# Gated linear attention block with a convolutional FFN: the gated product stored as four plain blocks, its sums formed by accumulating DMAs

## The chip, the cores and the metric

The kernel runs on one core of a Trainium2 chip. The metric is the device time of one execution in microseconds (us). Engines are called as in the profile: PE (matmuls) and PEld (its weight loads), DVE (vector), ACT (scalar), POOL (general vector), SP (an engine that here only issues DMAs). All data is float32.

## The reference

One layer over x of 2048 tokens by 1024 features: a gated linear attention mixer, then the FFN, each with a normalisation ahead of it and a residual behind it. The change lies in the FFN:

```python
def conv_ffn(h, w_up, conv_w, conv_b, w_down):       # h: 2048 x 1024
    u = causal_dwconv(h @ w_up, conv_w, conv_b)      # w_up: 1024 x 5632, 3 taps per feature
    g, val = jnp.split(u, 2, axis=-1)                # 2816 features each
    return (jax.nn.silu(g) * val) @ w_down           # w_down: 2816 x 1024

x = x + conv_ffn(rmsnorm(x, ffn_norm_w), ...)
return rmsnorm(x, final_norm_w)
```

## The kernel before, in words

Every large product is made of float32 operands that are split in two parts: `split` (L186 to L189) lets ACT cast the high part and DVE subtract it for the low part. `mm3p` (L174) then issues three matmuls of 128x512 for one block (L179, L180, L181). On top of that, each product of matrices is done as a fast 2x2 block product: seven products p1 to p7 of sums of blocks in place of eight.

The up stage (`phase_u`, ahead of and around L1237 to L1347) makes u = h @ w_up, the convolution, the gate and the gated product. Tokens come in two halves s of 1024, features in 11 pairs of tiles f; a half and a pair make a group of 7 products x 2 f = 14 jobs, each of 12 matmuls. There are 2 x 11 x 14 = 308 jobs, 3696 matmuls. One PSUM bank (`a`) collects p1, then p6, p7 and p4 of the same f on top of it, and ACT copies the intermediate states out: `copied` (L1237) copies p1 (tile c1) and p6 (c2), L1333 copies p7 (c3), L1340 copies p4. The next product into that bank waits for the copy. `conv` (L1247) forms the convolution on ACT (L1253) and DVE (L1255), `gated` (L1260) multiplies gate and value on DVE (L1262).

While the first half is worked on, the operands of the second half are prepared in steps (`prep_h2`, L820 ff.): each step makes the high and low part of a sum (tiles `h2p`, cast at L188, and stored from ACT at L841 into scratch `hd`), and at the change of halves SP loads them as `h_p` (L904). The tiles `h2p` (two per step), the c3 copies and the sums of the gated product share one ring of six buffers, tag "as" (AB = 6).

`gated` at an odd f has four quadrants of the pair: a11 and a21 (even f, two token quarters), a12 and a22 (odd f). It stores three of them plainly from SP and has POOL form four sums (L1276 add, L1280, L1278 and L1280 subtract) into the ring, each stored by SP (L1282). So scratch `ad` holds the seven operands of the down stage: 7 x 256 KB for each pair and half.

The down stage (L1351 ff.) runs 14 units, products p1, p5, p6, p7, p2, p4, p3, each for both halves; a unit has 11 steps q of 12 matmuls. Per step, SP loads a tile `da` of `ad` (`load_step`, 10 steps ahead of the matmuls, into a ring of four pairs of tiles), and `prep_step` splits it (tiles `da`, 4 steps ahead). In the unit of the first half the step also has weight blocks: SP loads them (L1380, tiles `dwr`, and L1357's `ch`), POOL sums them up (L1406 and L1408), and they are split into `dw_p`. The results go onto xs tiles, the residual rows, which SP loads during the first two units (L1464, 16 loads of 512 KB) and which DVE and POOL add to (L1489 to L1511). Final normalisation and output stand in the units p4 and p3 (L1466 to L1482).

A planner's clock decides when the delayed pieces (steps of `prep_h2`, weight preparation) are put into the code, and a scheduler orders each engine's instructions.

Of the kernel before, what the change touches and what calls it, by code (L numbers as in the profile page):

```python
# [10 lines left out]
F32 = mybir.dt.float32  # L11
# [3 lines left out]
ALU = mybir.AluOpType  # L15

P = 128
# [8 lines left out]
def hybrid_kernel(  # L26
# [17 lines left out]
    nc = tc.nc  # L44
    x = x[0]
# [19 lines left out]
    AB = 6  # L65
# [18 lines left out]
    NS = S // TS  # L84
    TT = TS // P
    PAIRS = TT // 2
    OPS = ("p1", "p5", "p6", "p7", "p4", "p2", "p3")

    PORD = ("p1", "p5", "p6", "p2", "p7", "p3", "p4")
    NQ = NF // 2  # L90
    ULEAD = 5
    DLEAD = 4
    DLOAD = 6
    DWLOAD = 3

    cst = ctx.enter_context(tc.tile_pool(name="cst", bufs=1))
    gx = ExitStack()
# [12 lines left out]
    pools = {}  # L110

    def scratch(shape, name):
        return dr.tile(shape, F32, tag=name, name=name)
# [7 lines left out]
    wsd = {(ps_, o, k): scratch([P, 2, 512], f"ws_{ps_}_{o}_{k}") for ps_ in "BY" for o in ("p5", "p6", "p7", "p3") for k in range(2)}  # L121
    b12d = [scratch([P, 512], f"b12_{j}") for j in range(NP)]
    hd = {(s, o, j): scratch([P, 2, 512], f"hd_{s}_{o}_{j}") for s in range(NS) for o in OPS for j in range(PAIRS)}
    ad = {(s, o, q): scratch([P, 512], f"ad_{s}_{o}_{q}") for s in range(NS) for o in OPS for q in range(NQ)}

    def mm_ps(name):
        return ps.tile([P, 512], F32, tag="mm", name=name, bufs=4)
# [4 lines left out]
    def raw_tile(shape, name):  # L132
        return wr.tile(shape, F32, tag="raw", name=name, bufs=RB)
# [757 lines left out]
    done = {"rows": 0}  # L891
# [290 lines left out]
    def tiles2(ap):  # L1182

        v = ap.rearrange("p (j c k) -> p c j k", c=2, k=P)
        return v[:, 0], v[:, 1]

    def tiles1(ap):
        return ap.rearrange("p (j k) -> p j k", k=P)
# [3 lines left out]
    def phase_u():  # L1192
        raws, wops, sums, made = {}, {}, {}, {}
# [46 lines left out]
        def new_u(s, i, f):  # L1240
            c = f + i * NF
            u = pools["us"].tile([P, TS + 2], F32, tag="u", name=f"u_{s}_{c}", bufs=3)
            nc.gpsimd.tensor_copy(u[:, 0:2], halo[:, c, :])
            made["u", i, f] = u
            return tiles2(u[:, 2:2 + TS])
# [14 lines left out]
        def gated(s, f):  # L1260
            t, v = made.pop(("t", 0, f)), made.pop(("t", 1, f))
            nc.vector.tensor_mul(t, t, v)  # L1262
            made["a", f % 2] = tiles2(t)
            q = f // 2
            if f % 2 == 0:
                nc.sync.dma_start(tiles1(ad[s, "p1", q]), made["a", 0][0])
                return
            (a11, a21), (a12, a22) = made["a", 0], made["a", 1]
            nc.sync.dma_start(tiles1(ad[s, "p2", q]), a12)
            nc.sync.dma_start(tiles1(ad[s, "p4", q]), a22)  # L1270
            last = None
            for o, fn, x, y in (("p5", "add", a21, a22), ("p6", "sub", None, a11), ("p3", "rsub", None, a12), ("p7", "sub", a11, a21)):
                t = pools["us"].tile([P, 512], F32, tag="as", name=f"as_{s}_{q}_{o}", bufs=AB)
                tv = tiles1(t)
                if fn == "add":
                    nc.gpsimd.tensor_add(tv, x, y)  # L1276
                elif fn == "rsub":
                    nc.gpsimd.tensor_sub(tv, y, last)  # L1278
                else:
                    nc.gpsimd.tensor_sub(tv, last if x is None else x, y)  # L1280
                last = tv
                nc.sync.dma_start(ad[s, o, q], t)  # L1282

        load(0, 0)
        load(0, 1)
# [1 line left out]
        done = 0  # L1287
        bank = {}
        for k, (s, g, o, f) in enumerate(jobs):
# [23 lines left out]
            if o == "p1":  # L1313
                a = bank["a", f] = mm_ps(f"ua_{s}_{f}")
# [5 lines left out]
            elif o == "p6":  # L1320
                a = bank["a", f]
                mm3p(a, pairs, first=False, more=True)
                made["u2", f] = copied(f"c2_{s}_{f}", a)
            elif o == "p2":
                pb = mm_ps(f"ub_{s}_{f}")
                mm3p(pb, pairs)
                ev, _ = new_u(s, 0, f)
                nc.vector.tensor_add(ev, tiles1(pb), tiles1(made.pop(("p1", f))))  # L1328
            elif o == "p7":
                a = bank["a", f]  # L1330
# [6 lines left out]
            elif o == "p4":  # L1337
                a = bank.pop(("a", f))
# [3 lines left out]
            else:  # L1342
                c = bank.pop(("c", f))
                mm3p(c, pairs, first=False, more=True)
                _, od = tiles2(made["u", 0, f][:, 2:2 + TS])
# [5 lines left out]
    units = [(o, s) for o in ("p1", "p5", "p6", "p7", "p2", "p4", "p3") for s in range(NS)]  # L1351
    steps = [(o, s, q) for o, s in units for q in range(NQ)]
    araw, wraw, aops, wops, chain, xs, acc, wgrp = {}, {}, {}, {}, {}, {}, {}, {}
    dstep = {"loaded": 0, "wloaded": 0, "done": 0}

    def blocks_of(o):
        return {"p1": (), "p5": ((1, 2),), "p6": ((2, 2),), "p7": ((2, 2), (1, 2)), "p2": ((2, 1),), "p4": ((2, 1),), "p3": ((2, 2),)}[o]  # L1357
# [16 lines left out]
    def load_wr(k):  # L1374
        o, s, q = steps[k]
        if s == 0:
            wraw[o, q] = []
            for ij in blocks_of(o):
                r = next(dstep["wr"])
                nc.sync.dma_start(r, block(q, *ij))  # L1380
                wraw[o, q].append(r)

    def load_step(k):
        o, s, q = steps[k]
        if k % 2 == 0:
            araw["tile"] = raw_tile([P, 2, 512], f"da_{o}_{s}_{q}")
        r = araw["tile"][:, k % 2, :]
        nc.sync.dma_start(r, ad[s, o, q])
        araw[o, s, q] = r

    def w_slots(o, q):
        if q % 4 == 0:
            wgrp[o] = slots(("p7", "p4", "p3")[q // 4], f"dw_{o}_{q}")
        return wgrp[o][q % 4 * 2:][:2]
# [22 lines left out]
    def d_load(n):  # L1417
        while dstep["wloaded"] < min(len(steps), n - DLOAD + DWLOAD):
            load_wr(dstep["wloaded"])
            dstep["wloaded"] += 1  # L1420
        while dstep["loaded"] < min(len(steps), n):
            load_step(dstep["loaded"])
            dstep["loaded"] += 1

    def d_prep(n):
        while dstep["done"] < min(len(steps), n):
            prep_step(dstep["done"])
            dstep["done"] += 1
# [55 lines left out]
    def use(o, s, m, pb, nw):  # L1484

        e, d = s * TT + 2 * m, s * TT + 2 * m + 1
        c1, c2 = slice(0, 512), slice(512, 1024)
        xe, xd = xs[e], xs[d]
        add = nc.vector.tensor_add  # L1489
        if o == "p1":  # L1490
            acc[s, m] = dx.tile([P, 512], F32, tag=f"acc{s}_{m}", name=f"acc_{s}_{m}")
            nc.scalar.copy(acc[s, m], pb)
            add(xe[:, c1], xe[:, c1], pb)
        elif o == "p5":
            add(xd[:, c2], xd[:, c2], pb)
            add(xe[:, c2], xe[:, c2], pb)
        elif o == "p6":
            add(acc[s, m], acc[s, m], pb)
            nc.gpsimd.tensor_add(xe[:, c2], xe[:, c2], acc[s, m])
        elif o == "p7":  # L1500
            add(acc[s, m], acc[s, m], pb)
            nc.gpsimd.tensor_add(xd[:, c1], xd[:, c1], acc[s, m])
            nc.gpsimd.tensor_add(xd[:, c2], xd[:, c2], acc[s, m])
        elif o == "p2":
            add(xe[:, c1], xe[:, c1], pb)
        elif o == "p4":
            add(xd[:, c1], xd[:, c1], pb)
            final_tile(d, nw)
        else:
            add(xe[:, c2], xe[:, c2], pb)  # L1510
            final_tile(e, nw)  # L1511

    nwf = dx.tile([P, D], F32, tag="nwf", name="nwf")
    more = [dx.tile([P, 512], F32, tag=f"wr{i}", name=f"dwr_{i}") for i in range(2 * (DWLOAD + 1) - len(dstep["wr"]))]
    dstep["wr"] = itertools.cycle(dstep["wr"] + more)
    for n, (o, s) in enumerate(units):
        banks = [(mm_ps if n % 2 == 0 else aux_ps)(f"pd_{o}_{s}_{m}") for m in range(PAIRS)]
        last = n + 1 == len(units)
# [8 lines left out]
        for q in range(NQ):  # L1527
            k = n * NQ + q
# [43 lines left out]
```

## Time and profile before

| | |
|---|---|
| time, 3 runs | 2183.61 us median, 2178.07 to 2184.76 |
| span of the profiled execution | 2176.4 us |
| mean granted clock of TensorE in it | 0.986 |
| up stage (first matmul into the second stage's) | 851.9 to 1743.0 us |
| down stage, matmuls | 1743.0 to 2167.9 us |
| stores of the gated product and its sums | 154 of 256 KB |
| loads of the down stage's operands | 154 of 256 KB |

The span lies 7.2 us below the median of the runs and 1.7 us below the lowest; it leaves out what lies ahead of the first and behind the last instruction. How to read the profile: busy time is summed by engine; a wait is put down to the instruction that released it last; the chain of waits follows the work that ended last back from its end. A window row gives the length, then busy time and count for PE, PEld, DVE, ACT and POOL, the granted clock, the busy share of the 16 DMA engines and GB/s.

### The profile page before, as it was taken

Reading aid. Unit: us, or ns where it says so; the run is one execution under the profiler, and the core shown is the slowest. Engines: PE = TensorE matmul, PEld = TensorE weight load, DVE = VectorE, ACT = ScalarE, POOL = GpSimd, SP = SyncE. Lnnn points to the kernel's source line nnn. Section 1 sums busy time; section 2 is a strip of 40 time slices with the busy share of each in tenths; the row PEclk is TensorE's granted clock in tenths of the full one; section 3 lists DMA queues with packets and bytes.
Section 4 is the critical chain, followed back from the end, with each engine's and each line's share of the span. In section 5 each row is a group of like instructions: output and inputs, shape, how many; then the busy total and the mean of one; then the engine's idle time right before and its main releaser. Section 6 shows DMA issues by size and latency. Waiting matters only on the chain.

```text
span 2176.4 us, 28914 instructions
## 1 busy us (share of the span) xinstructions
PE 2086.0 (96%) x9832; PEld 1730.6 (80%) x9832; DVE 1648.3 (76%) x2168; ACT 1104.3 (51%) x2024; POOL 734.9 (34%) x606
## 2 busy tenths in 40 slices
PE   7999999989998999799999998999999999999998
PEld 5788788878887887677888777888888877888886
DVE  8756888798888663778899776988888776457564
ACT  5555756665565775444554453554445533333342
POOL 2000011111111002456666554666565444037010
PEclk9999999999999999999999999999999999999999
DMA  6646684578557999654453458242424567254453
GB/s 219 223 165 211 213 297 137 159 229 298 178 195 251 323 344 365 207 163 131 146 184 102 146 177 291 88 131 76 139 77 124 187 247 269 97 184 160 141 182 113
DMA packets 305124, 411.76 MB, mean 189 GB/s; under 512 B 23742, under 2 KB 160110, under 8 KB 304976
## 3 DMA queue, kind: packets, MB, share of 16 engines
q1 hardware_dynamic: 267440, 346.99, 48.2%
q10 hardware_dynamic: 37536, 62.93, 8.6%
q8 instruction: 77, 1.26, 0.2%
q14 instruction: 71, 0.58, 0.1%
HBM read 266.70 MB, written 143.13 MB: 188 GB/s over the span
## 4 chain that ended last, share of the span: by engine, by line
PE 65%; DVE 13%; DMA 10%; issue 6%; ACT 2%; POOL 2%; SPq 0%; ACTq 0%; DVEq 0%; POOLq 0%
PE pd_p L180 5%; PE pd_p L181 5%; PE pd_p L179 5%; PE ua L179 5%; PE ua L180 5%; PE ua L181 5%; DVE t L1255 4%; DMA h_p<-hd_p 2%; PE uc L179 2%; PE uc L181 2%; PE uc L180 2%; PE mp_Y L180 2%; PE mp_Y L181 2%; PE mp_Y L179 2%; PE mp_R L179 2%
## 5 line engine op out<-in xcount | busy, mean ns | idle before, releaser
L179 PE MATMUL ua<-h_p,uw_p 128*128 128x512 f32 x704 | 279.0, 396 | 28.0 <-ACT c L1237 23.2
L1255 DVE SCALAR_TENSOR_TENSOR t<-u,cw,t 128x1024 f32<-128x1024 f32 x176 | 270.4, 1542 | 10.3 <-ACT t L1253 9.1
L180 PE MATMUL ua<-h_p,uw_p 128*128 128x512 f32 x704 | 277.7, 394 | 0.0
L181 PE MATMUL ua<-h_p,uw_p 128*128 128x512 f32 x704 | 277.2, 394 | 0.0
L180 PE MATMUL pd_p<-dw_p,da 128*128 128x512 f32 x616 | 240.7, 391 | 3.4 <-DVE da L189 3.4
L181 PE MATMUL pd_p<-dw_p,da 128*128 128x512 f32 x616 | 240.3, 390 | 0.0
L179 PE MATMUL pd_p<-dw_p,da 128*128 128x512 f32 x616 | 240.1, 390 | 0.0
L189 DVE TENSOR_TENSOR da<-da_p,da 128x512 fp32r<-128x512 f32 x154 | 131.4, 906 | 105.4 <-ACT da L188 105.3
L189 DVE TENSOR_TENSOR uw_p<-ur,uw_p 128x512 fp32r<-128x512 f32 x176 | 168.6, 979 | 48.8 <-ACT uw_p L188 48.4
L188 ACT CAST da<-da_p 128x512 fp32r<-128x512 f32 x154 | 85.3, 619 | 207.9 <-PE pd_p L181 149.9
L179 PEld LDWEIGHTS ua<-h_p,uw_p 128*128 128x128 f32 x704 | 134.4, 191 | 59.6 <-ACT c L1237 31.8
L188 ACT CAST uw_p<-us 128x512 fp32r<-128x512 f32 x132 | 82.1, 622 | 169.0 <-POOL us L1217 130.7
L189 DVE TENSOR_TENSOR uw_p<-us,uw_p 128x512 fp32r<-128x512 f32 x132 | 127.9, 978 | 47.8 <-ACT uw_p L188 46.8
L181 PEld LDWEIGHTS ua<-h_p,uw_p 128*128 128x128 f32 x704 | 134.5, 191 | 28.6
L180 PEld LDWEIGHTS ua<-h_p,uw_p 128*128 128x128 f32 x704 | 134.5, 191 | 27.9
L180 PEld LDWEIGHTS pd_p<-dw_p,da 128*128 128x128 f32 x616 | 116.0, 188 | 28.7 <-DVE da L189 4.7
L179 PE MATMUL uc<-h_p,uw_p 128*128 128x512 f32 x352 | 137.2, 390 | 0.9 <-DVE u L1328 0.9
L679 POOL TENSOR_TENSOR r<-r,gnw 128x512 f32<-128x512 f32 x32 | 46.9, 1466 | 268.6 <-ACT r L678 228.2
L181 PE MATMUL uc<-h_p,uw_p 128*128 128x512 f32 x352 | 136.9, 389 | 0.0
L180 PE MATMUL uc<-h_p,uw_p 128*128 128x512 f32 x352 | 136.9, 389 | 0.0
L181 PEld LDWEIGHTS pd_p<-dw_p,da 128*128 128x128 f32 x616 | 116.1, 188 | 24.1
L179 PEld LDWEIGHTS pd_p<-dw_p,da 128*128 128x128 f32 x616 | 116.1, 188 | 24.0
(278 smaller groups left out, 5474.8 us busy)
## 6 DMA issues: line engine op xcount, KB each, us to landing
ur<-in_ffn_w_up_dram SPq DMA_DIRECT2D x168, 256.0 KB, 3.7
da_p<-ad_p SPq DMA_DIRECT2D x154, 256.0 KB, 3.8
h_p<-hd_p SPq DMA_DIRECT2D x56, 512.0 KB, 8.0
ad_p<-as_p SPq DMA_DIRECT2D x88, 256.0 KB, 2.3
ad_p<-t SPq DMA_DIRECT2D x66, 256.0 KB, 3.1
x<-in_x_dram SPq DMA_DIRECT2D x32, 512.0 KB, 4.7
ch<-in_ffn_w_down_dram SPq DMA_DIRECT2D x61, 256.0 KB, 4.2
hr_A_p<-h1d_p SPq DMA_DIRECT2D x56, 256.0 KB, 3.0
```

The source lines that it names most:

```text
L179: nc.tensor.matmul(ps_ap, ah, bl, start=(first and i == 0), stop=False, **kw)
L180: nc.tensor.matmul(ps_ap, al, bh, start=False, stop=False, **kw)
L181: nc.tensor.matmul(ps_ap, ah, bh, start=False, stop=(last and i == len(pairs) - 1), **kw)
L188: nc.scalar.copy(hi, src)
L189: nc.vector.tensor_sub(lo, src, f32(hi))
L679: nc.gpsimd.tensor_mul(r, r, sp["gnw"])
L1255: nc.vector.scalar_tensor_tensor(t, u[:, k:k + TS], cw[:, k, c:c + 1], t, op0=ALU.mult, op1=ALU.add)
```

## The change

`gated` no longer makes sums. Every f stores its two quadrants plainly, so `ad` holds a11, a21, a12 and a22 from the up stage: four stores for a pair, and no POOL operation.

In the down stage, `load_step` loads the first addend. `add_step`, two steps behind the loads, lets POOL issue a DMA from `ad` into the same tile with the operation "add" (`accum_op`): p5 is a21 += a22, p6 is p5 += a11, p7 is a11 += a21, p3 is p6 += a12. `keep_step`, four steps behind the loads, stores the finished p5 and p6 back into `ad` from SP, since p6 and p3 start from them. The signs differ from before (all four are plain sums), and five operations in `use` become subtractions.

```diff
+    DADD = 2
+    DKEEP = 4
...
         def gated(s, f):
             t, v = made.pop(("t", 0, f)), made.pop(("t", 1, f))
             nc.vector.tensor_mul(t, t, v)
-            made["a", f % 2] = tiles2(t)
-            q = f // 2
-            if f % 2 == 0:
-                nc.sync.dma_start(tiles1(ad[s, "p1", q]), made["a", 0][0])
-                return
-            (a11, a21), (a12, a22) = made["a", 0], made["a", 1]
-            nc.sync.dma_start(tiles1(ad[s, "p2", q]), a12)
-            nc.sync.dma_start(tiles1(ad[s, "p4", q]), a22)
-            last = None
-            for o, fn, x, y in (("p5", "add", a21, a22), ("p6", "sub", None, a11), ("p3", "rsub", None, a12), ("p7", "sub", a11, a21)):
-                t = pools["us"].tile([P, 512], F32, tag="as", name=f"as_{s}_{q}_{o}", bufs=AB)
...
-                nc.sync.dma_start(ad[s, o, q], t)
+            for o, part in zip((("a11", "a21"), ("a12", "a22"))[f % 2], tiles2(t)):
+                nc.sync.dma_start(tiles1(ad[s, o, f // 2]), part)
...
+    ASRC = {"p1": ("a11",), "p5": ("a21", "a22"), "p6": ("p5", "a11"), "p7": ("a11", "a21"), "p2": ("a12",), "p4": ("a22",), "p3": ("p6", "a12")}
...
-        nc.sync.dma_start(r, ad[s, o, q])
+        nc.sync.dma_start(r, ad[s, ASRC[o][0], q])
         araw[o, s, q] = r
+
+    def add_step(k):
+        o, s, q = steps[k]
+        for other in ASRC[o][1:]:
+            nc.gpsimd.dma_start(araw[o, s, q], ad[s, other, q], accum_op=ALU.add)
+
+    def keep_step(k):
+        o, s, q = steps[k]
+        if o in ("p5", "p6"):
+            nc.sync.dma_start(ad[s, o, q], araw[o, s, q])
...
     def d_load(n):
...
+        for what, fn, late in (("added", add_step, DADD), ("kept", keep_step, DKEEP)):
+            while dstep[what] < min(len(steps), n - late):
+                fn(dstep[what])
+                dstep[what] += 1
```

On ACT, in the third group of the first half, the order before has two steps of the second half's operands (the casts into `h2p` and their stores) ahead of and between the two c2 copies of tiles f = 4 and 5:

```order
L188 CAST h2p_4_p6_0_10254<-h2r_4_0_9820 128x512
L188 CAST uw_0_4_p2_10337<-ur_0_4_1_10053 128x512
L841 DMA hd_1_p6_0_322<-h2p_4_p6_0_10254 128x512
L841 DMA hd_1_p6_0_322<-h2p_4_p6_1_10255 128x512
L188 CAST h2p_4_p2_0_10343<-h2r_4_1_9822 128x512
L1237 COPY c2_0_4_10335<-ua_0_4_10240 128x512
L188 CAST uw_0_5_p2_10358<-ur_0_5_1_10056 128x512
L841 DMA hd_1_p2_0_334<-h2p_4_p2_0_10343 128x512
L841 DMA hd_1_p2_0_334<-h2p_4_p2_1_10344 128x512
L1237 COPY c2_0_5_10356<-ua_0_5_10264 128x512
```

At the same place afterwards (line numbers are larger by two, and L1317 is the c3 copy) the rows are:

```order
L190 CAST uw_0_5_p4_10276<-ur_0_5_1_10023 128x512
L190 CAST uw_0_4_p2_10293<-ur_0_4_1_10020 128x512
L1239 COPY c2_0_4_10291<-ua_0_4_10196 128x512
L190 CAST uw_0_5_p2_10314<-ur_0_5_1_10023 128x512
L1239 COPY c2_0_5_10312<-ua_0_5_10220 128x512
```

The casts into `h2p` no longer stand between the c2 copies. On SP, in the second unit of the down stage, the order before is the loads of p5's operands, the xs rows and then the weight blocks `dwr`:

```order
L1464 DMA xs_13_16850<-x1d_13_91 128x1024
L1388 DMA da_p5_0_4_16845<-ad_0_p5_5_358 128x512
L1464 DMA xs_14_16868<-x1d_14_92 128x1024
L1388 DMA da_p5_0_6_16883<-ad_0_p5_6_359 128x512
L1464 DMA xs_15_16891<-x1d_15_93 128x1024
L1388 DMA da_p5_0_6_16883<-ad_0_p5_7_360 128x512
L1380 DMA dwr_0_16517<-in_ffn_w_down_dram 128x512
```

Afterwards the same stretch holds the stores of the sums (L1386), each of which waits for its accumulating DMA:

```order
L1386 DMA ad_0_p5_0_386<-da_p5_0_0_16508 128x512
L1465 DMA xs_13_16590<-x1d_13_91 128x1024
L1374 DMA da_p5_0_4_16583<-ad_0_a21_5_358 128x512
L1386 DMA ad_0_p5_1_387<-da_p5_0_0_16508 128x512
L1465 DMA xs_14_16610<-x1d_14_92 128x1024
L1374 DMA da_p5_0_6_16625<-ad_0_a21_6_359 128x512
L1386 DMA ad_0_p5_2_388<-da_p5_0_2_16544 128x512
L1465 DMA xs_15_16635<-x1d_15_93 128x1024
L1374 DMA da_p5_0_6_16625<-ad_0_a21_7_360 128x512
L1386 DMA ad_0_p5_3_389<-da_p5_0_2_16544 128x512
L1366 DMA dwr_0_16253<-in_ffn_w_down_dram 128x512
```

The load of step 5 now stands behind the store of step 0, and the first weight block behind the store of step 3. On POOL the accumulating DMAs (L1381) stand in one queue with the weight sums (L1403):

```order
L1381 DMA da_p5_0_2_16544<-ad_0_a22_3_378 128x512
L1403 TENSOR_TENSOR ch_0_16023<-ch_1_16024,ch_0_16023 128x512 x2
L1381 DMA da_p5_0_4_16583<-ad_0_a22_4_379 128x512
L1381 DMA da_p5_0_4_16583<-ad_0_a22_5_380 128x512
L1381 DMA da_p5_0_6_16625<-ad_0_a22_6_381 128x512
L1381 DMA da_p5_0_6_16625<-ad_0_a22_7_382 128x512
L1403 TENSOR_TENSOR ch_0_16023<-dwr_0_16253,ch_0_16023 128x512
```

The weight sum that uses the first block `dwr` stands behind the accumulating DMA of step 7.

More of the change, by code (lines that the diff above doesn't have):

```diff
@@ L123, in hybrid_kernel @@
     hd = {(s, o, j): scratch([P, 2, 512], f"hd_{s}_{o}_{j}") for s in range(NS) for o in OPS for j in range(PAIRS)}
-    ad = {(s, o, q): scratch([P, 512], f"ad_{s}_{o}_{q}") for s in range(NS) for o in OPS for q in range(NQ)}
+    ad = {(s, o, q): scratch([P, 512], f"ad_{s}_{o}_{q}") for s in range(NS) for o in ("a11", "a21", "a12", "a22", "p5", "p6") for q in range(NQ)}
     def mm_ps(name):
@@ L1262, in gated @@
             nc.vector.tensor_mul(t, t, v)
-            made["a", f % 2] = tiles2(t)
-            q = f // 2
-            if f % 2 == 0:
-                nc.sync.dma_start(tiles1(ad[s, "p1", q]), made["a", 0][0])
-                return
-            (a11, a21), (a12, a22) = made["a", 0], made["a", 1]
-            nc.sync.dma_start(tiles1(ad[s, "p2", q]), a12)
-            nc.sync.dma_start(tiles1(ad[s, "p4", q]), a22)
-            last = None
-            for o, fn, x, y in (("p5", "add", a21, a22), ("p6", "sub", None, a11), ("p3", "rsub", None, a12), ("p7", "sub", a11, a21)):
-                t = pools["us"].tile([P, 512], F32, tag="as", name=f"as_{s}_{q}_{o}", bufs=AB)
[L1274 to L1282, printed above, removed]
+            for o, part in zip((("a11", "a21"), ("a12", "a22"))[f % 2], tiles2(t)):
+                nc.sync.dma_start(tiles1(ad[s, o, f // 2]), part)
         load(0, 0)
@@ L1353, in hybrid_kernel @@
     araw, wraw, aops, wops, chain, xs, acc, wgrp = {}, {}, {}, {}, {}, {}, {}, {}
-    dstep = {"loaded": 0, "wloaded": 0, "done": 0}
+    dstep = {"loaded": 0, "wloaded": 0, "done": 0, "added": 0, "kept": 0}
+    ASRC = {"p1": ("a11",), "p5": ("a21", "a22"), "p6": ("p5", "a11"), "p7": ("a11", "a21"), "p2": ("a12",), "p4": ("a22",), "p3": ("p6", "a12")}
     def blocks_of(o):
@@ L1488, in use @@
         xe, xd = xs[e], xs[d]
-        add = nc.vector.tensor_add
+        add, sub = nc.vector.tensor_add, nc.vector.tensor_sub
         if o == "p1":
@@ L1495, in use @@
             add(xd[:, c2], xd[:, c2], pb)
-            add(xe[:, c2], xe[:, c2], pb)
+            sub(xe[:, c2], xe[:, c2], pb)
         elif o == "p6":
-            add(acc[s, m], acc[s, m], pb)
+            sub(acc[s, m], acc[s, m], pb)
             nc.gpsimd.tensor_add(xe[:, c2], xe[:, c2], acc[s, m])
@@ L1501, in use @@
             add(acc[s, m], acc[s, m], pb)
-            nc.gpsimd.tensor_add(xd[:, c1], xd[:, c1], acc[s, m])
-            nc.gpsimd.tensor_add(xd[:, c2], xd[:, c2], acc[s, m])
+            nc.gpsimd.tensor_sub(xd[:, c1], xd[:, c1], acc[s, m])
+            nc.gpsimd.tensor_sub(xd[:, c2], xd[:, c2], acc[s, m])
         elif o == "p2":
```

## The prediction

> **What bounds the kernel now.** I read the busy times first, then windows by stage, then the waits and the chains in the windows where matmuls are missing. The page says which engine the span belongs to:
>
> ```profile
> span 2176.4 us, 28914 instructions
> PE 2086.0 (96%) x9832; PEld 1730.6 (80%) x9832; DVE 1648.3 (76%) x2168; ACT 1104.3 (51%) x2024; POOL 734.9 (34%) x606
> ```
>
> PE is busy for 96% of the span, and the change leaves its matmuls as they are. So the change can only win stalls of PE and the slow matmuls behind a stall, or add some. Where they are, the windows show (length; busy and count of PE, PEld, DVE, ACT, POOL; granted clock; DMA share; GB/s):
>
> ```profile
> core 0: us, PE busy (x) PEld busy (x) DVE busy (x) ACT busy (x) POOL busy (x), PEclk, DMA share, GB/s
> 880.00:930.00 50.00, 43.37 (x179) 35.31 (x178) 38.07 (x39) 21.91 (x34) 24.33 (x21) 0.92 0.59 184
> 930.00:1330.00 400.00, 383.40 (x1660) 314.69 (x1659) 339.64 (x334) 197.78 (x300) 242.36 (x196) 0.98 0.50 158
> 1330.00:1380.00 50.00, 43.98 (x184) 35.68 (x183) 35.36 (x33) 21.77 (x34) 24.61 (x18) 0.93 0.57 176
> 1380.00:1730.00 350.00, 350.00 (x1546) 289.91 (x1545) 300.35 (x281) 173.54 (x260) 206.37 (x147) 1.00 0.37 113
> 1730.00:1830.00 100.00, 96.60 (x417) 78.91 (x416) 75.33 (x73) 40.90 (x69) 46.46 (x28) 0.98 0.75 271
> 1774.00:1806.00 32.00, 31.00 (x137) 25.37 (x136) 14.85 (x20) 9.23 (x17) 3.37 (x2) 1.00 1.02 389
> 1830.00:1930.00 100.00, 100.00 (x443) 82.80 (x442) 54.49 (x84) 31.12 (x57) 19.26 (x14) 1.00 0.49 161
> ```
>
> From 1380 to 1730 (second half of the up stage) nothing stalls: 1546 matmuls in 350 us, 4.417 per us at clock 1.00. Against that rate 880 to 930 lacks 42 matmuls (9.5 us), 930 to 1330 lacks 107 (24.2 us), 1330 to 1380 lacks 37 (8.4 us). In the down stage 1730 to 1830 lacks 26 against the 443 of 1830 to 1930 (5.9 us). The stretch 1774 to 1806 inside it is the only one where the DMA engines are full (share 1.02, 389 GB/s).
>
> **What PE waits for in the first half.** The waits from 918 to 1362 (total, times, longest):
>
> ```profile
> PE ua L179 <- ACT c L1237: 23.2, 8, 6.6
> ACT h2p_p L188 <- DMA ad_p<-as_p: 11.7, 3, 5.5
> ACT h2p_p L188 <- DMA hd_p<-h2p_p: 11.0, 2, 5.6
> PE ub L179 <- DMA h_p<-hd_p: 5.1, 1, 5.1
> ```
>
> PE waits for the ACT copies that free its bank. ACT is late because a cast into h2p stands ahead of the copy and waits for a ring buffer: three times for the store of a POOL sum (`as`), twice for the store of an earlier h2p. The chain into the stall at 1011 has the whole mechanism:
>
> ```profile
> 1004.54 1.67 POOL as_p L1276
> 1006.28 1.64 POOL as_p L1280
> 1007.93 2.26 DMA ad_p<-as_p
> 1010.21 0.62 ACT h2p_p L188
> 1010.83 0.49 ACT c L1237
> 1011.37 0.80 PE ua L179
> ```
>
> The second half prepares no h2p and has no such wait, though POOL forms the same sums there. The h_p wait is the change of halves:
>
> ```profile
> 1331.12 1.67 POOL as_p L1276
> 1336.19 1.71 POOL as_p L1280
> 1337.92 0.32 SPq L1282
> 1340.28 7.39 DMA h_p<-hd_p
> 1347.87 0.77 PE ub L179
> ```
>
> SP issues in order; the loads of h_p stand behind four stores that wait for four POOL sums.
>
> **Part 1: the sums leave the up stage.** What goes away on POOL and on SP:
>
> ```profile
> L1276 POOL TENSOR_TENSOR as_p<-t,t 128x512 f32<-128x512 f32 x22 | 36.8, 1673 | 26.6 <-DVE t L1262 26.6
> L1280 POOL TENSOR_TENSOR as_p<-as_p,t 128x512 f32<-128x512 f32 x22 | 35.7, 1621 | 1.7
> L1280 POOL TENSOR_TENSOR as_p<-t 128x512 f32<-128x512 f32 x22 | 35.4, 1609 | 0.0
> L1278 POOL TENSOR_TENSOR as_p<-t,as_p 128x512 f32<-128x512 f32 x22 | 35.4, 1609 | 1.6
> ad_p<-as_p SPq DMA_DIRECT2D x88, 256.0 KB, 2.3
> ad_p<-t SPq DMA_DIRECT2D x66, 256.0 KB, 3.1
> ```
>
> That is 143 us of POOL and 66 of 154 stores (88 plain ones remain). By themselves they are worth nothing, since POOL and DMA have room (POOL 242 of 400 us, DMA share 0.50 in 930 to 1330). What counts is the ring: four of its tiles per group disappear, so a cast into h2p no longer waits for `ad_p<-as_p`, and it finds a buffer that was released several steps earlier, which covers the 5.6 us waits for `hd_p<-h2p_p` too. The order after also has the casts out from between the c2 copies. At the change of halves h_p no longer waits for 1331.12 to 1337.9, four sums of 1.7 us, so it lands some 6 us earlier; the wait was 5.1.
>
> The loss there is 24.2 + 8.4 = 32.6 us. What is late next are the copies behind ordinary ACT and DVE work, which in the second half cost nothing; I leave 3.6 us for what remains and take **29 us**. Lower bound 18: half of the 24.2 (the three `as` waits are about half of the five) and 6 of the 8.4. Upper bound 36: all, and 3 of the 9.5 us before 930. That first stall I otherwise leave in, for the order ahead of it is unchanged.
>
> **Part 2: the sums enter the down stage's DMA.** Loads stay 154. New are 88 accumulating DMAs (22 each for p5, p6, p7, p3) and 44 stores of kept sums. The units p5 to p7 (66 steps) carry 66 and 44 of these, and this is where the rows are tight:
>
> ```profile
> 1743.02 0.39 PE L179 MATMUL pd_p<-dw_p,da 128*128 128x512 f32 x1
> 1784.53 0.32 SPq L1388 DMA_DIRECT2D da_p<-ad_p  x1
> xs<-x1d SPq DMA_DIRECT2D x16, 512.0 KB, 8.3
> ```
>
> A step is 12 / 4.417 = 2.717 us. The matmuls of p1 start at 1743.0 and take 22 steps, so p5 starts at 1802.8 and p7 ends at 1982.1. The first operand of p5 is loaded at 1784.53. Splitting lies ahead of the matmuls, so the last operand of p7 must be there about 8 us before its end: a window of 190 us. A 256 KB tile costs the full engines 262,144 / 389,000 = 0.674 us. Work in the window: 70 loads (four of them p2's, ahead), 44 kept sums and 48 weight blocks are 162 tiles, 109.2 us; nine xs rows (seven issued after 1784.53, two in flight) and the final norm's weights, 20 tiles in all, 13.5 us. Sum 122.7 us, to which 66 accumulating DMAs come at A each.
>
> No accumulating DMA is in this trace. Lower bound of A: one pass like a load, 0.674. Upper bound: three passes (read, read again, write, each like a transfer), 2.02. I take two passes, 1.35: nearest to a load and a store of the same tile, since source and old value are both read and the result written once. Then 122.7 + 89.0 = 211.7, 22 us over the window. Before has already lost 5.9 us at this place, so **16 us** are new. At 0.674 the sum is 167 and fits; at 2.02 it is 256, and 60 us are new.
>
> The Trainium skill speaks against the change here: "Collectives: The Full Stack", section "The bandwidth ceiling: the fold count and why AG ≠ RS ≠ AR", says that a reduction in the DMA engine pushes two source reads through the same read ring and so runs at about half the rate of a copy (measured ratio 1.93). As an estimate from that page, A would be 0.674 x 1.93 = 1.30, the new loss about 13 us and the time 2167; no run yet shows it.
>
> **Part 3: order and waits.** `keep_step` has SP wait for an accumulating DMA, and behind it are queued the next load, the xs rows and the weight blocks. The weight blocks matter most, since the stall at 1823 follows from them:
>
> ```profile
> 1799.49 7.74 DMA dwr<-in_ffn_w_down_dram
> 1807.30 1.29 POOL ch L1406
> 1813.60 3.79 DMA dwr<-in_ffn_w_down_dram
> 1823.56 0.79 PE pd_p L180
> ```
>
> The first block moves behind the store of step 3's sum. That step's load was issued near 1790 and takes about 8 us; its accumulating DMA then needs between 4 and 8, which gives an issue at 1802 to 1806 in place of 1799.5. SP's silence meanwhile empties the queue, which returns a part. Priced alone: 2 to 8 us, taken 4; beside the 16 us above it is the same lateness and not counted again.
>
> Issuing from POOL costs between 0.32 us (SP's issue) and 1.67 us (a POOL sum). 66 of them are 21 to 110 us in 180; POOL is busy for 19 of 100 us from 1830 on, so even the upper end is covered there. Turning five additions of `use` into subtractions, and the stage p3 with its 22 accumulations but only 11 weight blocks, I cost at nothing: PE's lead over 22 steps (60 us) covers 22 x (0.674 + 1.35) + 7.4 = 52 us.
>
> **Sum.** Profiled execution: 2176.4 - 29 + 16 = 2163; it lies 7.2 us below the median of the runs, so **2171 us** against 2183.6.
>
> **Rivals.**
>
> *The accumulation is as cheap as a load* (A up to about 1.0). For it: outside 1774 to 1806 the share is 0.49, the engines have room. Then only part 3's 4 us remain: 2183.6 - 29 + 4 = 2159. Chance 0.33.
>
> *The DMA becomes the bound of the down stage* (slower than before). Mechanism: in p5 to p7 each tile takes three passes, loads and kept sums wait, and PE waits for `da`. It decides from 66 A = 190 - 122.7 + 5.9 + 29, A = 1.55; at 2.02 the time is 2183.6 - 29 + 60 = 2215. For it: the loaded queue at 1784 to 1806 already gives 8 us per load, and a load of step 5 now follows a finished accumulation of step 0. Against: from 1830 on half the engines' time is free. Chance 0.20.
>
> *The up stage keeps half of its stalls.* Two of five h2p waits were for `hd_p<-h2p_p`, not for a sum; if the ring only rotates to the next such wait, the gain is 14: 2183.6 - 14 + 16 = 2186. Against: the second half with the same sums and no h2p is free of stalls, and the ring now has four tiles fewer per group. Chance 0.12.
>
> **How the numbers follow.** The forecast (A near two passes) has 0.35. A measurement of this kernel can tell about 0.3%, 6.5 us. Faster by more: nearly all of the first rival (0.32), three quarters of the forecast (0.26): 0.58. Within: 0.07 of the forecast, 0.06 of the half gain, 0.03 of the dear accumulation just above its turning point: 0.16. Slower: the rest, 0.26. The range goes from 2153 (cheap accumulation with some 34 us of gain) to 2206 (A about 1.9); the forecast's own range is 2162 to 2180.
>
> **What would show it.** Up stage: the waits `PE ua <- ACT c` of the first half under 4 us, no wait for `h_p`, and 930 to 1330 with about 1750 matmuls. Down stage: a DMA share near 1.0 from 1784 up to about 1970, PE waiting for `da` or `dw` by some 20 us, and the busy time of the queue that POOL issues on, divided by 88 and by a load's, gives A. The forecast is wrong if that ratio is near 1 or 3, if c copies still wait for h2p casts, or if PE waits for POOL while the DMA engines are idle.

## The result, and the profile after

The changed kernel takes 2192.66 us (median of 5 runs, 2190.66 to 2196.57) against 2178.07 us for the kernel before beside it: ratio 1.0065, 95% interval 1.0048 to 1.0082, slower by 14.6 us. Forecast were 2171 us, faster. The time lies inside the stated range, on the wrong side. The times of all runs are medians; that of e5 leaves out two of its ten executions, of 2591 and 8690 us.

The up stage did what was forecast, and more. From 918 to 1362 the copies that free PE's bank hold PE for 0.6 us, where they held it for 23.2:

```profile
PE ua L181 <- ACT c L1239: 0.6, 1, 0.6
```

The first matmul of the down stage, at 1743.02 before, is now here:

```profile
1704.08 0.39 PE L181 MATMUL pd_p<-dw_p,da 128*128 128x512 f32 x1
```

That is 38.9 us earlier. The windows of the changed kernel (same columns as before) show where the gain and the loss lie:

```profile
880.00:930.00 50.00, 47.99 (x205) 39.20 (x204) 39.62 (x42) 25.74 (x40) 23.63 (x20) 0.97 0.53 159
930.00:1330.00 400.00, 400.00 (x1767) 331.31 (x1766) 330.48 (x352) 207.14 (x312) 188.92 (x167) 1.00 0.50 156
1330.00:1380.00 50.00, 49.39 (x218) 40.60 (x217) 38.56 (x42) 27.60 (x42) 19.13 (x17) 1.00 0.45 127
1774.00:1830.00 56.00, 50.48 (x207) 40.53 (x206) 30.32 (x36) 15.95 (x28) 28.39 (x26) 0.94 0.99 271
1830.00:1930.00 100.00, 76.63 (x305) 59.80 (x303) 40.40 (x51) 24.68 (x43) 37.18 (x38) 0.90 0.92 239
1930.00:1980.00 50.00, 43.09 (x170) 34.72 (x171) 28.78 (x29) 12.80 (x23) 31.59 (x31) 0.90 0.96 241
```

From 930 to 1330 PE is busy all the time, with the 1767 matmuls of the full rate. The loss is in the units p5 to p7: 305 matmuls where 443 fit, at a clock of 0.90, with the DMA engines at 0.92 (from 1830 to 1930). The page has a queue that was not there:

```profile
span 2189.3 us, 28925 instructions
...
q0 software_dynamic: 12672, 23.07, 6.3%
...
da_p<-ad_a POOLq DMA_DIRECT2D x88, 256.0 KB, 5.8
```

The 88 accumulating DMAs took 6.3% of 2189.3 us, so 1.57 us of all 16 engines each. From 1830 to 1930 both queues can be compared (packets, MB, share):

```profile
q1 hardware_dynamic: 9078, 16.53, 46.8%
q0 software_dynamic: 4032, 7.34, 44.8%
```

16.53 MB are 63 plain tiles, 0.742 us each; 7.34 MB are 28 accumulating ones, 1.60 us each. And SP, which loads, waits (1800 to 1980, its own queue; then PE from 1743 on):

```profile
SPq L1386 <- DMA da_p<-ad_a: 71.8, 29, 6.4
```

```profile
PE pd_p L181 <- ACT da L190: 20.3, 8, 8.1
PE pd_p L182 <- DVE da L191: 18.1, 7, 5.8
```

SP spends 71.8 of 180 us waiting with a store of a kept sum for the accumulation, and PE waits for the split of the operands that SP then loads late.

### The profile page after: what moved, and what is told of

The parts are those of the page before. It is cut to its first block, busy times and chain, and to the rows that moved or that the text cites. A ratio compares the mean times of both kernels' runs of the same rounds, so it can differ in the third digit from the quotient of the medians.

```text
span 2189.3 us, 28925 instructions
## 1 busy us (share of the span) xinstructions
PE 2091.3 (96%) x9832; PEld 1732.0 (79%) x9832; DVE 1563.8 (71%) x2168; ACT 1111.3 (51%) x2024; POOL 647.0 (30%) x606
## 4 chain that ended last, share of the span: by engine, by line
PE 65%; DMA 12%; DVE 10%; issue 6%; POOL 2%; ACT 2%; SPq 1%; ACTq 0%; DVEq 0%; POOLq 0%
PE ua L181 6%; PE ua L182 6%; PE ua L183 6%; DMA da_p<-ad_a 5%; PE uc L181 3%; PE uc L183 3%; PE uc L182 3%; PE pd_p L182 3%; PE pd_p L181 3%; PE pd_p L183 3%; PE mp_Y L183 2%; PE mp_Y L182 2%; PE mp_Y L181 2%; PE mp_R L181 2%; PE mp_R L182 2%
## 5 line engine op out<-in xcount | busy, mean ns | idle before, releaser
L181 PE MATMUL pd_p<-dw_p,da 128*128 128x512 f32 x616 | 246.1, 400 | 20.3 <-ACT da L190 20.3
L182 PE MATMUL pd_p<-dw_p,da 128*128 128x512 f32 x616 | 246.1, 400 | 18.1 <-DVE da L191 18.1
L1257 DVE SCALAR_TENSOR_TENSOR t<-u,cw,t 128x1024 f32<-128x1024 f32 x176 | 254.1, 1446 | 11.4 <-ACT t L1255 10.4
L183 PE MATMUL pd_p<-dw_p,da 128*128 128x512 f32 x616 | 244.9, 398 | 0.0
L191 DVE TENSOR_TENSOR uw_p<-ur,uw_p 128x512 fp32r<-128x512 f32 x176 | 123.1, 716 | 73.5 <-ACT uw_p L190 68.4
L191 DVE TENSOR_TENSOR uw_p<-us,uw_p 128x512 fp32r<-128x512 f32 x132 | 121.8, 932 | 63.7 <-ACT uw_p L190 63.3
L181 PEld LDWEIGHTS pd_p<-dw_p,da 128*128 128x128 f32 x616 | 118.9, 193 | 48.5 <-ACT da L190 23.7
L182 PEld LDWEIGHTS pd_p<-dw_p,da 128*128 128x128 f32 x616 | 119.1, 193 | 46.9 <-DVE da L191 21.9
L1255 ACT ACTIVATE t<-u,cw 128x1024 f32<-128x1024 f32 x88 | 109.8, 1248 | 58.7 <-DVE u L1330 58.6
L183 PEld LDWEIGHTS pd_p<-dw_p,da 128*128 128x128 f32 x616 | 118.7, 193 | 24.8
```

The source lines that it names most:

```text
L181: nc.tensor.matmul(ps_ap, ah, bl, start=(first and i == 0), stop=False, **kw)
L182: nc.tensor.matmul(ps_ap, al, bh, start=False, stop=False, **kw)
L183: nc.tensor.matmul(ps_ap, ah, bh, start=False, stop=(last and i == len(pairs) - 1), **kw)
L191: nc.vector.tensor_sub(lo, src, f32(hi))
L1255: nc.scalar.activation(t, u[:, 2:2 + TS], AF.Identity, scale=cw[:, 2, c:c + 1], bias=cw[:, 3, c:c + 1])
L1257: nc.vector.scalar_tensor_tensor(t, u[:, k:k + TS], cw[:, k, c:c + 1], t, op0=ALU.mult, op1=ALU.add)
```

## The experiments

Two theories of the down stage were tried against each other: **engine time** (accumulating DMAs and kept sums need more time of the DMA engines than p5 to p7 last) and **order** (SP waits for a finished sum, with the next loads behind it in its queue). A third question was what in the up stage had made the stalls. Runs without an interval are single times.

**e1: plain DMAs in place of the accumulating ones.**

```diff
-            nc.gpsimd.dma_start(araw[o, s, q], ad[s, other, q], accum_op=ALU.add)
+            nc.gpsimd.dma_start(araw[o, s, q], ad[s, other, q])
```

> The changed kernel with the 88 accumulating DMAs made into plain loads of the same block into the same tile, still issued by POOL behind the same waits (the second addend replaces the sum, so the operands of p5, p6, p7 and p3 are not sums). Theory 1, engine time: an accumulating tile holds all 16 DMA engines for 1.58 us in the trace of after (28.8% of 482 us, 88 tiles), a plain one for 0.75 us, and the units p5 to p7 ask for more than their matmuls last. Then 66 x 0.83 = 55 us of engine time go, the rest fits, and the time is about 2145 us (2138 to 2155). Theory 2, order: the loss comes from SP waiting in its queue for the finished sum before the next loads, and from POOL waiting for the load. All these waits remain here, each shorter by 1 to 2 us: the time stays above 2172 us.

Measured 2144.35 us, as engine time had it. But the plain DMA lands sooner too: SP's wait for it from 1800 to 1980 fell from 71.8 to 47.6 us. POOL idles less ahead of its DMAs as well (see "POOL and p3" below). So the run says that the accumulation matters, not by which of these ways.

**e2: neither accumulations nor kept sums** (both functions return at once; p6 and p3 load a21).

> The changed kernel with neither accumulating DMAs nor stores of kept sums (the operands of p5, p6, p7 and p3 are then only their first addend). Both theories: only the up stage's gain is left. The profile of after has the down stage begin 38.9 us earlier, so 2139 us (2134 to 2144), with the DMA engines about half busy in the down stage. If the down stage still stalls, something else than the sums costs there.

Measured 2133.6 us, 0.4 us off the expected band. The down stage has no stall at all. Everything that the changed kernel loses there, 59.1 us against this run, comes from the sums and their stores.

**e3: the kept sums not stored** (`keep_step` returns; p6 and p3 start from a21).

> The changed kernel with all 88 accumulating DMAs but without the 44 stores of kept sums (p6 and p3 start from a21, so their operands lack an addend). Theory 1, engine time: 44 x 0.75 = 33 us of engine time less in p5 to p7, so some 17 of the 50 us of loss stay: about 2158 us (2150 to 2168). Theory 2, order: SP no longer waits for any sum, the loads run ahead as before, and the loss goes: below 2147 us.

Measured 2153.54 us, between the two numbers but in the band of engine time. So 88 accumulations alone cost 19.9 us over e2, the 44 stores (with the waits that they bring) another 39.1.

**e4: accumulations in the first half of the tokens alone.** In the second half POOL forms the sums as before:

```diff
+            if s == 0:
+                return
...
+            for o, x, y in (("p5", a21, a22), ("p6", None, a11), ("p3", None, a12), ("p7", a11, a21)):
+                t = pools["us"].tile([P, 512], F32, tag="as", name=f"as_{s}_{q}_{o}", bufs=AB)
...
-        for other in ASRC[o][1:]:
+        for other in () if s else ASRC[o][1:]:
...
```

> The changed kernel in the first half of the tokens; in the second half POOL forms the four sums in the up stage as before and SP stores them, so the down stage has 44 accumulating DMAs (33 in p5 to p7) and 22 kept sums. The whole computation is done. Theory 1, engine time: 33 x 1.58 + 22 x 0.75 = 69 us less of engine time in p5 to p7, which then fit: the gain of the up stage stays nearly whole, 2143 us (2137 to 2152), faster than both. Theory 2, order: the waits of the first half's units remain, half of the loss stays: about 2165 us.

Measured 2155.24 us, ratio to before 0.9883 (0.9852 to 0.9914): faster than both kernels, 3 us above the band of engine time and 10 below the other number. The window of its remaining loss:

```profile
1774.00:1806.00 32.00, 24.39 (x93) 18.85 (x92) 14.61 (x20) 11.10 (x21) 14.36 (x13) 0.84 1.02 321
```

93 matmuls where 142 fit (11 us), with the engines full: here p5's first sums meet the loads of xs rows and weight blocks.

**e7: kept sums stored from ACT** (`nc.scalar.dma_start` in `keep_step`).

> The changed kernel with the 44 stores of kept sums issued by ACT instead of SP, so that no load and no weight block stands behind a wait for a sum on SP (ACT's casts do). Nothing is left out. Theory 1, engine time: the same bytes through the same 16 DMA engines, so the time stays within 8 us of 2192. Theory 2, order on SP: SP runs ahead again, and a good part of the 50 us returns: below 2175 us.

Measured 2208.2 us, neither number. SP no longer waits for a sum, but now casts on ACT wait, from 1743 to 1983:

```profile
ACT da L190 <- DMA ad_p<-da_p: 65.7, 5, 19.9
PE pd_p L181 <- ACT da L190: 32.3, 10, 7.5
```

ACT's casts feed PE directly, and the stores with their waits now stand between them. The run does not tell the theories apart.

**e9: the kept store replaced by a copy that waits for nothing** (`nc.sync.dma_start(ad[s, o, q], ad[s, "a21", q])`).

> The changed kernel, where each of the 44 stores of kept sums is made into a copy of the stored block a21 into the same place, DRAM to DRAM, from SP at the same place in its queue (p6 and p3 then start from a21 alone). The bytes through the DMA engines stay; SP waits for no sum. Theory 1, engine time: time stays near the changed kernel's, 2192 (2178 to 2198). Theory 2, order on SP: as without the stores, 2154 (2146 to 2166).

Measured 2155.93 us, the number of the order theory, but the run does not say that. The copies had no one to wait for, and the scheduler put them far ahead, the first into the up stage:

```profile
926.65 1.40 SPq L1386 DMA_DIRECT2D ad_p<-ad_a  x2
```

So bytes and waits had both left p5 to p7, as in e3. Inconclusive.

**e11: the same wait with few bytes.**

```diff
...
-            nc.sync.dma_start(ad[s, o, q], araw[o, s, q])
+            nc.sync.dma_start(ad[s, o, q][:, 0:16], araw[o, s, q][:, 0:16])
```

> The changed kernel, where each of the 44 stores of kept sums writes 16 of the 512 columns (8 KB in place of 256 KB); it stands at the same place of SP's queue and waits for the same sum (p6 and p3 start from a21 alone). The waits stay, the bytes go. Theory 1, engine time (the stores' 33 us on the full DMA engines): as without the stores, 2154 to 2160 us. Theory 2, order (SP's waits for the sums): as the changed kernel, above 2180 us. Between 2160 and 2180 both have a part.

Measured 2179.89 us, at the upper edge of the band in which both theories have a part. With 8 KB in place of 256 KB the stores still cost 26.4 of the 39.1 us. Not all of this is waiting: from 1830 to 1930 the 22 short stores take, by an estimate from the plain queue's 35.1 us for 10.98 MB at 0.742 us per 256 KB, some 0.2 us of the DMA engines each, up to 9 us for all 44. From 1800 to 1980 SP's wait, and the window 1830 to 1930:

```profile
SPq L1386 <- DMA da_p<-ad_a: 65.3, 29, 7.3
```

```profile
1830.00:1930.00 100.00, 84.30 (x334) 66.94 (x333) 47.36 (x60) 26.71 (x46) 41.39 (x43) 0.90 0.87 194
```

334 matmuls in place of 305, while the engines move 194 GB/s instead of 239. Engine time as the only cause had fallen here.

**e13: DKEEP = 6** (no other edit) and **e14: e4 with DKEEP = 6.**

> The changed kernel with DKEEP = 6 instead of 4, nothing left out: SP's store of a sum (and with it the wait for the sum) stands behind the load of six steps later. Order theory (a load of step k + 5 follows the finished sum of step k, and that loop of load, POOL's issue, accumulation and SP takes about as long as its five steps of 2.72 us): the loop now spans seven steps, 19 us, and no longer binds; left are the engine time of sums and stores, 2134 + 20 + 13 = 2167 us (2158 to 2176). Engine time alone: bytes and passes are the same, 2192 us (2186 to 2198). If the wait only moves to the ring of raw tiles (a load needs the store of eight steps before to have landed), also near 2190.

> e4 (sums in the DMA for the first half of the tokens alone) with DKEEP = 6, nothing left out. Order theory: of e4's 21 us above the kernel without any sums, the 14 us at 1782 to 1793 come from SP waiting for the first sums while weight blocks stand behind; about half returns, 2148 us (2142 to 2154). Engine time alone: unchanged, 2155 us.

Measured 2194.99 us (ratio 1.0078, 1.0058 to 1.0098) and 2154.41 us (0.9886, 0.9870 to 0.9903): no gain in either; e13 lies in the band of engine time alone. The order shows that neither run tested what it was meant to test. The distance on SP, in steps, from the store of a kept sum to the last load ahead of it is 3 to 6 in the first half of the tokens of p5 and 4 to 6 for the first four steps of p6; after that both the changed kernel and e13 have 3, 2, 1, 0 in groups of four. The changed kernel has in p6:

```
L1374 DMA da_p6_0_6_17093<-ad_0_p5_6_392 128x512
L1386 DMA ad_0_p6_2_399<-da_p6_0_2_17018 128x512
L1374 DMA da_p6_0_6_17093<-ad_0_p5_7_393 128x512
L1386 DMA ad_0_p6_3_400<-da_p6_0_2_17018 128x512
L1386 DMA ad_0_p6_4_401<-da_p6_0_4_17056 128x512
L1386 DMA ad_0_p6_5_402<-da_p6_0_4_17056 128x512
L1386 DMA ad_0_p6_6_403<-da_p6_0_6_17093 128x512
L1386 DMA ad_0_p6_7_404<-da_p6_0_6_17093 128x512
L1374 DMA da_p6_0_8_17138<-ad_0_p5_8_394 128x512
```

The source puts the store four steps behind the loads; the scheduler moved the next loads behind the stores, so that SP waits for the sum of the tile it has just loaded before it loads another. On the chip that is a loop, in the chain at 1893 to 1908 of the changed kernel:

```profile
1893.36 5.66 DMA da_p<-ad_a
1899.04 0.32 SPq L1386
...
1899.45 3.38 DMA da_p<-ad_p
...
1904.17 0.72 POOL da_p L1381
...
1908.24 5.24 DMA da_p<-ad_a
```

```profile
1885.19 1.82 SPq L1374 DMA_DIRECT2D da_p<-ad_p  x4
1893.07 6.29 SPq L1386 DMA_DIRECT2D ad_p<-da_p  x4
1899.45 1.40 SPq L1374 DMA_DIRECT2D da_p<-ad_p  x2
```

From one accumulation to the next lie 14.9 us: landing 5.66, SP 0.4, load 3.4, POOL 5.4 with its waits. The second piece, SP's time line, shows loads in groups of four, stores in groups of four; four steps of matmuls last 10.9 us.

**e16: the same kernel with the order forced.**

```diff
...
+            tc.add_manual_dep(kept.ins, loads[k + 4].ins.name, mybir.DependencyInfo(mybir.DependencyClass.NoSync, mybir.DependencyReason.DATA), reason="order")
```

> The changed kernel, nothing left out, with an order dependency added: the store of the kept sum of step k stands on SP behind the load of step k + 4, as the source has it. The scheduler had undone that: from step 32 on it put up to eight stores in a row, the last one straight behind the load of its own step (distances 3, 2, 1, 0), in the changed kernel and in e13 alike. Order theory: with distance 4 kept everywhere, SP waits less and the loads run on while sums land; of the 26 us that e11 put on the waits the larger part returns: 2172 us (2162 to 2180). Engine time alone: the same bytes and passes, 2192 us (2186 to 2198).

Measured 2171.16 us, ratio 0.9964 (0.9951 to 0.9977): 21.5 us below the changed kernel, with every byte, sum and store in place. From 1800 to 1980, and the window:

```profile
SPq L1387 <- DMA da_p<-ad_a: 41.7, 22, 5.7
```

```profile
1830.00:1930.00 100.00, 88.06 (x364) 70.58 (x362) 52.49 (x63) 29.14 (x50) 47.20 (x48) 0.94 1.05 284
```

The wait fell from 71.8 to 41.7 us, and only now are the engines really full (1.05, 284 GB/s against 239). Order cost 21.5 us; what is left over e2, 37.6 us, goes with full engines, though SP still waits for sums there and no run takes those waits away while the bytes stay in p5 to p7.

**e17: distance 6.**

> As e16 with distance 6 (DKEEP = 6). Order theory: a sum has two more steps to land, 2168 us (2158 to 2176), or back up to 2180 if loads now wait for the stores to free the raw tiles (a tile is loaded again eight steps later). Engine time alone: 2192 us (2186 to 2198).

Measured 2196.43 us (1.0076, 1.0052 to 1.0101), outside both bands of the order theory and inside that of engine time alone. But from 1830 to 1930 PE loses a third of its matmuls (311 of 443) at a share of the DMA engines of 0.85, so in that stretch it is not the engines that bind. The rival wait that the expectation named came in a larger size; from 1800 to 1980 SP waits with a load for the store that frees the raw tile:

```profile
SPq L1375 <- DMA ad_p<-da_p: 87.9, 18, 6.4
```

A ring of eight steps must hold load, sum and store; a store four steps behind fits, one six behind doesn't.

**e18: e4 with the order forced.**

> e4 (accumulating DMAs for the first half of the tokens alone) with the order dependency of e16, nothing left out. In e4 the first unit's distances are 4 already and only p6's were 0 to 3; its stalls lie in the first unit. Order theory: only the 4 us at 1917 return, 2151 us (2146 to 2156); the 14 us at 1782 to 1793 are the engines' time where sums, xs rows and weight blocks meet. If they were waits of SP as well, below 2146.

Measured 2151.64 us (0.9864, 0.9843 to 0.9884), as expected; the interval overlaps with e4's. From 1774 to 1806 it has the same 93 matmuls and a share of 1.04: the loss there does not come from what the scheduler undid, for in e4 too stores and loads alternate there. Whether SP's waits at that distance have a part in it, this run cannot say; e3, where no sum is stored, has 102 matmuls there at a share of 0.91.

**The up stage: e5 and e6, sums in place.** POOL writes the sums over the quadrants; in e6 POOL itself stores those of the first half's last group.

```diff
...
+            for o, fn, out_, x, y in (("p5", "add", a22, a21, a22), ("p7", "sub", a21, a11, a21), ("p6", "sub", a11, a22, a11), ("p3", "sub", a12, a12, a11)):
+                (nc.gpsimd.tensor_add if fn == "add" else nc.gpsimd.tensor_sub)(out_, x, y)
+                nc.sync.dma_start(tiles1(ad[s, o, q]), out_)
```

> The kernel before with one change: POOL writes the four sums over the quadrants of the gated product themselves instead of into the ring that they share with the tiles h2p. All 88 POOL sums, all 154 stores and the whole computation stay; the down stage is that of before. Theory ring: the stalls of the first half come from the shared ring alone, so they vanish although POOL and the queues do the same work; only the wait for h_p at the change of halves (some 8 us with its slow matmuls) stays, since the sums still stand ahead of it on SP. 2180 - 30 = 2150 us (2144 to 2156). Rival, POOL's load: the sums slow DVE and ACT beside them or fill the queues, and ACT stays late: above 2168 us.

> As e5, and the four stores of the sums of the first half's last group are issued by POOL, so that SP reaches the loads of h_p without waiting for POOL. The whole computation is done. Theory ring and queue: the wait for h_p goes too, another 6 to 8 us: 2143 us (2138 to 2149), the up stage as short as in the changed kernel and the down stage as in the kernel before. If the h_p wait had another cause, the time equals that of e5.

Measured 2172.48 us (0.9983, 0.9965 to 1.0001) and 2173.11 us (0.9982, 0.9971 to 0.9994): both miss their number by more than 20 us, and e5 lies where its rival had it. In the waits of e5 from 918 to 1362 no cast into h2p waits for a store any more, but there is a new wait:

```profile
POOL t L1272 <- DMA ad_p<-t: 52.2, 9, 7.3
...
PE ua L179 <- ACT c L1237: 18.2, 10, 7.1
```

Writing over a quadrant needs its store to have landed; POOL stands still for that, and its weight sums with it. The edit took one wait away and put another in, so it did not test the ring.

**e8: the sums in a tile of their own, not stored.**

> The kernel before with its 88 POOL sums at the same places, but into one tile of their own, and without the 88 stores of the sums (the down stage loads the stored p1 block in place of p5, p6, p7 and p3, so their operands are stand-ins). The ring of h2p and c3 has the sums no longer, POOL waits for no store, POOL's work is that of before. Theory ring (the sums' place in the shared ring, and their stores ahead of h_p, made the stalls): the up stage gets as short as in the changed kernel, 2139 us (2133 to 2148). Rival, POOL's load (143 us of POOL work that stands ahead of the weight sums for which ACT waits): ACT stays late in the first half, above 2155 us.

Measured 2139.71 us, as the ring theory had it (the sums' place in the ring and their stores, which this run takes away together). POOL is busier than in the kernel before, and the stalls are gone:

```profile
930.00:1330.00 400.00, 400.00 (x1766) 331.21 (x1765) 357.96 (x348) 208.38 (x314) 251.36 (x204) 1.00 0.47 150
```

One stall stays, the first (6.6 us at 922), which the changed kernel shortened to 2.0. POOL's work stays here and went there; that it is the cause was not tested by itself.

**e10: e4, and the first half's p5 summed by POOL too.**

> As e4 (accumulating DMAs in the first half of the tokens alone), and the first half's p5 too is summed by POOL in the up stage and stored (one ring tile per group instead of four); 33 accumulating DMAs and 11 kept sums remain. The whole computation is done. In e4 the stalls that are left lie at 1782 to 1793, where p5's first accumulations meet the loads of xs and of weights. Theory 1, engine time: 11 x 1.58 + 11 x 0.75 = 26 us less of engine time in just that stretch, so most of the 14 us lost there return, and one tile per group leaves the ring free enough: 2144 us (2138 to 2150). Theory 2, order: the same direction, some 5 us. If one sum per group already brings the stalls of the up stage back: above 2157 us.

Measured 2158.94 us (0.9906, 0.9889 to 0.9924), the case above 2157 us. Between 1774 and 1806 it does have 136 matmuls instead of 93, so the collision is gone. But stalls of the up stage are back (1708 matmuls from 930 to 1330), and not through the ring. The chain into the one at 1198:

```profile
1197.07 0.69 DVE h2p_p L191
...
1197.78 0.39 ACTq L843
...
1198.22 0.59 ACT c L1239
...
1198.86 0.80 PE ua L181
```

ACT issues the store of an h2p that waits for DVE's low part, and the copy stands behind it: the scheduler had put the steps of h2p between the copies again.

**e12 and e15: a ring of two for the sums.** e12 is the kernel before with this ring (and AB = 5, and 512 instead of 1024 bytes for the descriptors of POOL's DMAs, which makes room); in e15 POOL also stores the sums of the first half's last group.

```diff
-                t = pools["us"].tile([P, 512], F32, tag="as", name=f"as_{s}_{q}_{o}", bufs=AB)
+                t = pools["us"].tile([P, 512], F32, tag="own", name=f"as_{s}_{q}_{o}", bufs=2)
```

> The kernel before with the four POOL sums in a ring of two buffers of their own (the ring of h2p and c3 has five instead of six). All sums and stores stay as before, the down stage too, nothing is left out. Theory ring: a cast into h2p no longer meets a sum, so the six stalls of the first half mostly go: 2146 us (2138 to 2156), with the wait for h_p still there. POOL waits for the store of two sums before, about 1 us for each of two sums per group; if that holds up POOL's weight sums as much as in e5, the time stays above 2165 us.

> e12 (POOL sums in a ring of their own) with the four sums of the first half's last group stored by POOL, so that SP reaches the loads of h_p without them; nothing left out. Theory: the stall of 4 us at 1320 and its slow matmuls go: 2144 us (2139 to 2150), the fastest complete version. If that stall had another cause, as e12, 2150.

Measured 2150.14 us (0.9861, 0.9838 to 0.9884) and 2148.10 us (0.9863, 0.9849 to 0.9878): the whole computation without any accumulating DMA, faster than before by 1.4% and than the changed kernel by some 2%. e12 from 930 to 1330:

```profile
930.00:1330.00 400.00, 392.02 (x1719) 323.04 (x1718) 361.78 (x345) 204.40 (x308) 244.01 (x199) 1.00 0.54 174
```

1719 matmuls against 1660 before. e15's time lies inside the band that its theory gave, but it cannot be told from e12's, and the stall that was to go did not: at the change of halves PE waits 4.4 us for h_p, as the kernel before did for 5.1. What holds h_p there was not followed further.

## Why the prediction was wrong, point by point

**The up stage: right mechanism, too small.** Forecast 29 us, at most 36; measured 38.9. By windows at 4.417 matmuls per us: 107 more from 930 to 1330 (24.2 us), 34 more to 1380 (7.7), 26 more from 880 to 930 (5.9). I had left 3.6 us for "what remains" and nothing for the first stall; the first went, and of the second 2.0 of 6.6 us stayed. e8 shows that the shared ring, with the stores behind it, made the stalls after 930, and in e12, which keeps every store and gives the sums a ring of their own, the waits for c copies behind the first stall fall from 16.6 to 2.3 us.

**The price of an accumulation: right ratio, wrong base.** "Two passes" holds: 1.60 against 0.742 us for a plain tile in the same stretch, a factor of 2.2 (1.57 on the mean of all 88). In e1 POOL issues the same 88 DMAs without the addition, and the page has for them:

```profile
q0 software_dynamic: 7040, 23.07, 3.3%
```

That is 3.3% of 2142.7 us, 0.80 us each: it is the addition that doubles the price, not the queue. The rule of the Trainium skill, "Collectives: The Full Stack", section "The bandwidth ceiling: the fold count and why AG ≠ RS ≠ AR", about half the rate of a copy (1.93, measured there on a collective's reduce-scatter against its all-gather), agrees in kind. But I had taken 0.674 us for a tile from 1774 to 1806, where 15 xs rows of 512 KB were loaded beside 17 tiles of 256 KB; with tiles of 256 KB alone it is 0.742 (0.739 from 1830 to 1930 in e1, where nothing accumulates). With these prices the same sum gives 162 x 0.742 + 13.5 + 66 x 1.60 = 239 us for a window of 190: 49 us over it, 43 of them new, where 16 were forecast. e16, with the order forced, loses 37.6 us against e2, which has no stall there. Without the kept stores the sum is 118 x 0.742 + 13.5 + 66 x 1.60 = 207 us, 17 over the window; e3 loses 19.9.

**The step that failed: order and waits.** The prediction priced the waits of `keep_step` at "2 to 8 us, taken 4", "the same lateness and not counted again". The order alone is worth 21.5 us in e16: with it forced the kernel runs in 2171.16 us, faster than before. I had read the order at p5's first steps, where the distance is 4 as in the source, and taken that for all of p5 to p7. The loop at distance 0, 14.9 us for four steps, stands later in the order, and a count of distances ahead of the result would have shown it.

Put together: -38.9 us in the up stage, +31.7 in the down stage with the order forced (the 37.6 of e16 less the 5.9 that the kernel before lost there) and +21.5 for the order make +14.3, against 14.6 measured. The forecast had -29, +16 and nothing. Its 16 was thus too small as well, by half; either loss alone would have left the kernel faster, and the two together did not. That e16 comes out at the forecast's 2171 us is luck: the gain was forecast too small by 10 us, the loss at the engines by 16, and the forecast started from 2183.6 us, 5.5 above the kernel before that ran beside the result. Luck too is that the measured time lies in the range, whose upper end stood for A of about 1.9.

**POOL and p3.** POOL's time line and its waits (1743 to 2189) in the changed kernel, and PE's time line in p3:

```profile
1799.67 0.86 POOL L1381 DMA_DIRECT2D da_p<-ad_a  x1 [2.00 <-issue]
```

```profile
POOL da_p L1381 <- issue: 47.9, 27, 4.9
```

```profile
2129.16 0.79 PE L181 MATMUL pd_p<-dw_p,da 128*128 128x512 f32 x1 [2.61 <-ACT da L190]
```

An issue costs POOL 0.86 us, inside the bounds; but POOL also waited 47.9 us ahead of accumulating DMAs for nothing that the trace names. In e1, with plain DMAs at the same places, this is 4.1 us, so it comes with the addition. The loss does not follow it: e3 has 59.3 us of it and loses 19.9 us against e2, e16 has 40.5 and loses 37.6. What it is stays open. p3, costed at nothing, has a stall of 2.6 us, and e2 has none.

**The rivals.** Cheap accumulation is out. The slower side had its place right (p5 to p7) and its turning point, A = 1.55, almost met by 1.57; the second mechanism added to it made the difference. That the up stage keeps half of its stalls is out as well.

## What to carry to other kernels

A store that waits for a transfer holds every load behind it on the same queue; count how many loads stand between, step by step through the whole stage, because a scheduler may undo the distance that the source has. A DMA that adds cost about two plain ones of engine time here, so moving sums from an engine with room to the DMA pays only where the DMA has room as well. When a stall comes from a shared ring, a small ring for one of the sharers (e12) was cheaper here than moving its work away.

## What was not expected of the hardware

The busy share of the DMA engines misled: at 0.87 (e11) and 0.92 (the changed kernel) PE waited for a loop of waits, and the bytes of the changed kernel ran at 1.05 and 284 GB/s once the order was forced (e16). And a price per byte does not carry from one mix of transfers to another: 389 GB/s at a share of 1.02, with xs rows of 512 KB among the loads, make 0.674 us for 256 KB, where tiles of 256 KB took 0.742. That the larger rows make this difference was not tested by itself. Last, the addition itself brought idle time on POOL: 47.9 us with it, 4.1 without it (e1).
